# A hybrid mLSTM and delta-rule block: high and low part of the tokens in one moving operand of 512 columns

## The chip, the cores and the metric

The kernel runs on one core of a Trainium2 chip. The metric is the time of one execution on the device in microseconds (us); lower is better. "PE" is TensorE, "DVE" is VectorE, "ACT" is ScalarE, "POOL" is GpSimd and "SP" is SyncE, which issues most of the loads.

## What is computed

One layer of a bidirectional block on 256 tokens of width 2048, all in fp32:

```
h    = RMSNorm(x) * (1 + scale_m) + shift_m          # scale, shift, gates from silu(c) @ ada_w
proj = h @ w_in                                      # 2048 x 18512
y_a  = (sigmoid(a_o) * norm(biMLSTM(a_q, a_k, a_v, gates))) @ w_branch_a
qkv  = silu(conv5(b_qkv))                            # centred depthwise convolution, 5 taps
y_b  = (norm(biGatedDelta(qkv, gates)) * silu(b_z)) @ w_branch_b
x    = x + gate_m * ((g_a * y_a + g_b * y_b) @ w_out)
x    = x + gate_f * SwiGLU(RMSNorm(x) * (1 + scale_f) + shift_f)
out  = RMSNorm(x)
```

The delta rule (GDN) has 16 heads of width 128, the mLSTM 4 heads with keys of 256 and values of 512.

## The kernel before

A product of two fp32 matrices is made of three products in the faster type fp32r. Each operand is split into a high part (rounded to fp32r) and a low part (what is left): `hh` and `hl` for the tokens, `wh` and `wl` for the weights. The sum is hh·wh + hl·wh + hh·wl. For weights, ACT makes `wh` by a copy and DVE makes `wl` by a subtraction.

There are two kinds of job for a product with weights:

- `tjob`: the tokens are stationary (128 of them at a time), the weights move, 512 columns in one pass. It serves the projections that stay by token (z, v, o and the merge gates `ma`, `mb`), and later all products of the branches and the FFN.
- `fjob` (products by feature): the weights are stationary, 128 features at a time, and the 256 tokens move. The result is 128 features x 256 tokens in one half of a PSUM bank of 512 fp32. Its contraction over 2048 runs in 16 blocks, two halves of 8, and each half is one step of the job. Of these jobs there are 36 for q, k and v of the GDN heads 4 to 15 (`b_job`, tiles `acc_b`, `raw_b`, `wh_b`, `wl_b`) and 13 for q and k of the mLSTM heads (`a_qk`, tiles `acc_a` and so on). Heads 0 to 3 are made differently, in the first stage, by the product of L564 (`first`), which works on the unsplit fp32 `x`.

`woven` reorders the columns of the moving operand, so that the two halves of the tokens alternate. What is in the bank is therefore in alternating order, and the eviction reads it with a stride of two.

What follows an `fjob` is its `done`. For a GDN head that is `gdn_conv`: ACT copies the bank into `pad` (L336); ACT makes the middle tap of the convolution, `cv` (L339); DVE adds four more taps to it (L341); and later, as a function kept back in `behind` and called by `settle`, ACT makes the activation (L344) into `kq` or `vf`. `gdn_phase1` of the head takes these up: PE transposes `vf` (L612, tile `vps`), ACT squares `kq`. For the mLSTM, `keep_f` copies the bank into `ev` (L365, shown as `ev_a`), and ACT issues the store of it to DRAM.

The stages: first x is normalised and the first heads are made (to about 200 us). Then, to about 810 us, the GDN heads are worked through in groups of four. Their chain of small steps (phase 1, inversion, blocks, phase 2) would leave PE idle, so jobs are pulled in between: `stream` runs the b jobs of the next two heads and `fill` takes steps of the jobs in `rest`, in numbers written out by hand (`second`, `after`, `last`). Meanwhile `ada_parts` loads the rest of the modulation weights, 1 MB at a time, and DVE reduces each against the row of silu(c) (L114, 2.29 us each). From 965 us on follow the branches' products, the merge and the FFN, which have no `fjob`.

The order on PE is near that of the program. The order on DVE and ACT is fixed when the kernel is built, by a planner that goes by the order of the program, by when each instruction could start, and by its own costs; `order(...)` pins an instruction to its place in the program. Each engine then works its queue strictly in that order.

Of the kernel before, what the change touches and what calls it, by code (L numbers as in the profile page):

```python
# [10 lines left out]
F32R = mybir.dt.float32r  # L11
AF = mybir.ActivationFunctionType
ALU = mybir.AluOpType
PSUM = bass.MemoryType.PSUM

P = 128
T = 256
D = 2048
KB = D // P
# [6 lines left out]
GRP = 4  # L26
# [26 lines left out]
def hybrid_block(ctx: ExitStack, tc: tile.TileContext, xr, nfr, crow, pk_d, cst_d, ada2, ada4, win0, winb, wint, wba, wbb, wo, wgu, wd, out, dbg=None):  # L53
    nc = tc.nc
    V, S, G, PE = nc.vector, nc.scalar, nc.gpsimd, nc.tensor

    def pool(stack, name, bufs=1, **kw):
        return stack.enter_context(tc.tile_pool(name=name, bufs=bufs, **kw))
# [4 lines left out]
    g_ps = pool(ctx, "g_ps", 4, space=PSUM)  # L63
    sa, sx, sf = ExitStack(), ExitStack(), ExitStack()
    crp = pool(ctx, "crp")
    bigA = pool(sa, "bigA", 2, side="right")

    def big(p, dt, name):
        return p.tile([P, KB, T], dt, tag="b16", name=name)
# [106 lines left out]
    def fjob(name, src, done):  # L176

        ps = acc_ps.tile([P, 512], F32, tag="acc", name=f"acc_{name}")
        o = ps[:, :T]
        raw = raw_tile([P, KB, P], f"raw_{name}")  # L180
        nc.sync.dma_start(raw, src)
        for k0 in range(0, KB, 8):
            wh = st.tile([P, 8, P], F32R, tag="wh", bufs=3, name=f"wh_{name}_{k0}")
            wl = st.tile([P, 8, P], F32R, tag="wl", bufs=3, name=f"wl_{name}_{k0}")
            S.activation(wh, raw[:, k0 : k0 + 8], AF.Copy)  # L185
            settle()
            V.tensor_tensor(wl, raw[:, k0 : k0 + 8], wh.bitcast(F32), ALU.subtract)  # L187
            for k in range(8):
                kk = k0 + k
                PE.matmul(o, wh[:, k], woven(hh[:, kk]), start=kk == 0, stop=False)  # L190
                PE.matmul(o, wh[:, k], woven(hl[:, kk]), start=False, stop=False)  # L191
                PE.matmul(o, wl[:, k], woven(hh[:, kk]), start=False, stop=kk == KB - 1)  # L192
            if k0:
                pump()
                done(o.rearrange("p (c h) -> p h c", h=2))
            yield True

    def woven(a, n=2):

        return a.rearrange("p (h c) -> p c h", h=n)  # L200
# [95 lines left out]
    inst_d = [tc.dram_tile([64, 32, 32], F32, name=f"inst_d{g}") for g in range(NH_B // GRP)]  # L296
    inv_d = [tc.dram_tile([32, 4, 16, 32], F32, name=f"inv_d{g}") for g in range(NH_B // GRP)]

    hh = big(bigA, F32R, "hh")
    hl = big(bigA, F32R, "hl")  # L300

    evp = pool(sa, "evp", side="right")
    fr = pool(sf, "fr", side="right")
# [6 lines left out]
    for i in range(NP_):  # L310
        pd = fr.tile([P, T + 4], F32, name=f"pad{i}")
# [7 lines left out]
        order(G.memset(al[:, :, 0:8], 0.0))  # L319
        order(G.dma_start(al[:, :, 8:], alpha_d[:, h].partition_broadcast(P)))  # L320

    def gdn_conv(h, j, ps):

        if j == 0:
            kq = fr.tile([P, 2, T], F32, tag="kq", bufs=2, name=f"kq{h}")
            vf = fr.tile([P, T], F32, tag="vf", bufs=2, name=f"vf{h}")
            parts[h] = (kq, vf)
            if h == 1:
                decay_load(h)
        kq, vf = parts[h]  # L330
        cb = (16 + h, h, 32 + h)[j]
        w = [pk[:, PK_CONV + 5 * cb + i : PK_CONV + 5 * cb + i + 1] for i in range(5)]
        pd = pads[npad[0] % NP_]
        npad[0] += 1
        if ps is not None:
            S.activation(pd[:, 2 : T + 2].rearrange("p (h c) -> p h c", h=2), ps, AF.Copy)  # L336
        settle(1)
        cv = fr.tile([P, T], F32, tag="cv", bufs=2, name=f"cv{h}_{j}")
        S.activation(cv, pd[:, 2 : T + 2], AF.Copy, scale=w[2])  # L339
        for i in (0, 1, 3, 4):  # L340
            V.scalar_tensor_tensor(cv, pd[:, i : i + T], w[i], cv, ALU.mult, ALU.add)  # L341

        def end():
            order(S.activation(kq[:, j] if j < 2 else vf, cv, AF.Silu))  # L344
            if ps is None:
                evict(3 * h + j + 1 + NP_)

        behind.append(end)
# [11 lines left out]
        return done  # L360

    def keep_f(dst, name):
        def done(ps):
            ev = evp.tile([P, T], F32, tag="evf", bufs=2, name=f"ev_{name}")
            S.activation(ev.rearrange("p (h c) -> p h c", h=2), ps, AF.Copy)  # L365
            S.dma_start(dst, ev)
        return done

# [5 lines left out]
        return tjob(f"z{g}", [wint[g, u] for u in range(4)], hh, hl, done, early)  # L374

    def b_job(h, j):
        return fjob(f"b{h}_{j}", winb[3 * (h - GRP) + j], lambda ps: gdn_conv(h, j, ps))

    def a_qk(h, j):
        return fjob(f"a{h}_{j}", winb[36 + 4 * h + j], keep_f(kq_d[h][j], f"a{h}_{j}"))  # L380
# [115 lines left out]
    with ExitStack() as s0:  # L496
        w0 = pool(s0, "w0")

        x = w0.tile([P, KB, T], F32, name="x")
        ss = w0.tile([P, 2], F32, name="ssx")  # L500
        rows = w0.tile([P, T], F32, name="rows")
        xt = []
        for t in range(2):
            xt.append(w0.tile([P, D + 2], F32, tag="ra", bufs=5, name=f"xt{t}"))
            order(nc.sync.dma_start(xt[t][:, :D], xr[:, t]))

        junk = hl.rearrange("p b t -> p (b t)")
        c_row(0)
        order(S.activation(junk[:, :D], xt[0][:, :D], AF.Square, accum_out=ss[:, 0:1]))
        for g in (1, 2, 3):  # L510
            c_row(g)
        order(V.scalar_tensor_tensor(junk[:, D : 2 * D], xt[1][:, :D], 1.0, xt[1][:, :D], ALU.mult, ALU.mult, accum_out=ss[:, 1:2]))
        order(S.activation(ss, ss, AF.Sqrt, bias=epsc, scale=1.0 / D))

        def loads(b):
            ra = [w0.tile([P, D + 2], F32, tag="ra", bufs=5, name=f"ra{b}_{i}") for i in range(2)]
            raw = st.tile([P, N0, P], F32, tag="raw", bufs=3, name=f"raw0_{b}")
            for i in range(2):
                order(nc.sync.dma_start(ra[i], ada2[b, :, i]))
            order(nc.sync.dma_start(raw, win0[b]))  # L520
            return ra, raw

        def scale(b, ra):
            m2 = w0.tile([P, 2], F32, tag="m2", bufs=3, name=f"m2_{b}")
            f = pk[:, PK_NMIX + b : PK_NMIX + b + 1]
            order(V.scalar_tensor_tensor(ra[0], ra[0], f, row_c, ALU.mult, ALU.mult, accum_out=m2[:, 0:1]))
            return m2

        def shift(ra, m2):
            order(V.scalar_tensor_tensor(ra[1], ra[1], 1.0, row_c, ALU.mult, ALU.mult, accum_out=m2[:, 1:2]))  # L530

        ra, raw = loads(0)
        m2 = scale(0, ra)
        order(V.reciprocal(ss, ss))
        dg = w0.tile([P, T], F32, name="dgx")
        for t in range(2):
            order(V.tensor_scalar(dg[:, t * P : (t + 1) * P], ident, ss[:, t : t + 1], None, ALU.mult))
        shift(ra, m2)
        for b2 in range(KB // 2):
            px = gps(f"pxx{b2}")  # L540
            for e in range(2):
                for t in range(2):
                    order(PE.transpose(px[:, e * T + t * P : e * T + (t + 1) * P], xt[t][:, (2 * b2 + e) * P : (2 * b2 + e + 1) * P], ident))
            order(S.activation(x[:, 2 * b2 : 2 * b2 + 2], px.rearrange("p (e t) -> p e t", e=2), AF.Copy))
        prow = acc_ps.tile([P, 512], F32, tag="acc", name="prow")
        order(PE.matmul(prow[:, :T], ones, dg, start=True, stop=True))
        order(S.activation(rows, prow[:, :T], AF.Copy))
        banks = [acc_ps.tile([P, 512], F32, tag="acc", name=f"first{i}") for i in range(4)]
        banks += [gps(f"first{i}") for i in range(4, 8)]
        first = [banks[o // 2][:, (o % 2) * T : (o % 2 + 1) * T] for o in range(N0)]  # L550
        for b in range(KB):
            if b:
                ra, raw = loads(b)
                m2 = scale(b, ra)
            order(V.scalar_tensor_tensor(x[:, b], x[:, b], m2[:, 0:1], rows, ALU.mult, ALU.mult))
            if b:
                shift(ra, m2)
            order(S.activation(x[:, b], x[:, b], AF.Identity, bias=m2[:, 1:2]))  # L558
            order(S.activation(hh[:, b], x[:, b], AF.Copy))
            for bb in ((b - 1,) if b < KB - 1 else (b - 1, b)):  # L560
                if bb >= 0:
                    order(V.tensor_tensor(hl[:, bb], x[:, bb], hh[:, bb].bitcast(F32), ALU.subtract))
            for o in range(N0):
                PE.matmul(  # L564
                    first[o], raw[:, o], x[:, b], start=b == 0 and o % 2 == 0, stop=b == KB - 1 and o % 2 == 1
                )


        zj = z_job(0, 3)
        next(zj)  # L570
        fills[:] = [zj] + rest
        zz = w0.tile([P, T], F32, name="zz")
        for i, _ in enumerate(gates(w0, zz, first)):
            fill(2 if i in (2, 3, 4, 6, 8, 9, 10) else 1)
# [707 lines left out]
    left, right = slice(0, 256), slice(256, 512)  # L1282
# [120 lines left out]
    for j in range(FB // 4):  # L1403
# [4 lines left out]
        for e2 in range(2):  # L1408
            px = gps(f"pxf{j}_{e2}")
            for e in range(2):  # L1410
                f = 2 * e2 + e
                for t in range(2):
                    PE.transpose(px[:, e * T + t * P : e * T + (t + 1) * P], sg[:, t, f * P : (f + 1) * P], ident)
            b = 4 * j + 2 * e2
# [35 lines left out]
    for g in range(4):  # L1450
        c = slice(g * 512, (g + 1) * 512)
# [119 lines left out]
```

## Time and profile before

| what | before |
|---|---|
| time, median of 3 runs | 1991.46 us (1991.42 to 1999.04) |
| the profiled execution | 1994.34 us, span 1992.4 us |
| PE busy (matmuls) | 1937.3 us, 97% of the span |
| weight loads of PE (PEld) | 1708.8 us, 86% |
| DVE busy | 1407.0 us, 71% |
| ACT busy | 1032.8 us, 52% |
| POOL busy | 116.4 us, 6% |
| share of PE in the chain that ended last | 76% |
| granted clock of PE | 0.991 |

"Busy" counts the time in which at least one instruction of the engine is under way. Matmuls overlap one another, so the duration of one is longer than the interval at which they start; the interval is what a product costs when many follow each other. A line such as `L190 PE MATMUL acc_b<-hh,wh_b 128*128 128x256 f32 x576 | 163.4, 284 | 0.4 <-ACT wh_b L185 0.4` means: line 190, on PE, output `acc_b` from `hh` and `wh_b`, weights of 128x128, output 128x256, 576 times; 163.4 us busy, 284 ns on average; PE was idle for 0.4 us before them, waiting for ACT's `wh_b`. In a list of waits, "PEld vps L612 <- ACT vf L344: 11.5, 8, 4.8" means that the weight loads of L612 waited for ACT's `vf` for 11.5 us in all, 8 times, at most 4.8 us. In a timeline the first two numbers are the start and the duration in us.

### The profile page before, as it was taken

What the parts mean: (1) busy time and instruction counts of PE and PEld (TensorE: products, weight loads), DVE (VectorE), ACT (ScalarE), POOL (GpSimd) and SP (SyncE); (2) the same over time, 40 slices, a digit from 0 to 9 for tenths busy, and PEclk for the clock granted to TensorE, in tenths of its full rate; (3) what the DMA queues carried; (4) which work ended last, traced back from release to release, by engine and by line L of the source; (5) the groups of instructions that cost most, each with busy time, mean ns of one, the idle gap of its engine ahead of it and who ended that gap; (6) DMA issues with size and microseconds to landing.
All of it is one profiled execution on the core that took longest, in us unless ns stands there. A gap on an engine that the chain in (4) does not pass through costs nothing.

```text
span 1992.4 us, 27101 instructions
## 1 busy us (share of the span) xinstructions
PE 1937.3 (97%) x10418; PEld 1708.8 (86%) x10418; DVE 1407.0 (71%) x2067; ACT 1032.8 (52%) x1557; POOL 116.4 (6%) x211
## 2 busy tenths in 40 slices
PE   8999999999999999999999999999999999999998
PEld 6878889998898899889787888888888888888886
DVE  6778887887878798867476878765666665555554
ACT  3137647765666576555444544554444444444444
POOL 0001210111001101010100000200000000000000
PEclk9999999999999999999999999999999999999999
DMA  9987676655667666587786888566676675565653
GB/s 399 420 338 232 190 250 231 222 182 199 232 191 231 222 235 210 197 278 265 255 303 230 351 300 325 176 239 247 235 268 237 234 269 194 200 212 201 210 194 145
DMA packets 78962, 485.64 MB, mean 244 GB/s; under 512 B 10585, under 2 KB 15969, under 8 KB 24433
## 3 DMA queue, kind: packets, MB, share of 16 engines
q1 hardware_dynamic: 63216, 450.69, 62.6%
q0 software_dynamic: 8160, 17.88, 4.0%
q10 hardware_dynamic: 7458, 15.36, 2.0%
q8 instruction: 81, 1.33, 0.3%
q14 instruction: 47, 0.39, 0.1%
HBM read 467.07 MB, written 16.82 MB: 243 GB/s over the span
## 4 chain that ended last, share of the span: by engine, by line
PE 76%; DVE 10%; DMA 8%; ACT 2%; issue 2%; POOL 0%; ACTq 0%; SPq 0%; DVEq 0%; POOLq 0%
PE acc_gt L238 4%; PE acc_gt L237 4%; PE acc_gt L239 4%; PE acc_up L238 4%; PE acc_up L237 4%; PE acc_up L239 4%; PE acc_d L237 4%; PE acc_d L238 4%; PE acc_d L239 4%; DMA ra<-ada 3%; PE acc_o L239 2%; PE acc_o L237 2%; PE acc_o L238 2%; DMA ada<-ada 2%; PE acc_b L190 2%
## 5 line engine op out<-in xcount | busy, mean ns | idle before, releaser
L218 DVE TENSOR_TENSOR wl_d<-raw_d,wh_d 128x1024 fp32r<-128x1024 f32 x88 | 107.7, 1225 | 105.9 <-ACT wh_d L216 105.9
L218 DVE TENSOR_TENSOR wl_up<-raw_up,wh_up 128x1024 fp32r<-128x1024 f32 x88 | 107.7, 1225 | 100.3 <-ACT wh_up L216 100.3
L218 DVE TENSOR_TENSOR wl_gt<-raw_gt,wh_gt 128x1024 fp32r<-128x1024 f32 x88 | 108.2, 1229 | 79.6 <-ACT wh_gt L216 79.5
L190 PE MATMUL acc_b<-hh,wh_b 128*128 128x256 f32 x576 | 163.4, 284 | 0.4 <-ACT wh_b L185 0.4
L192 PE MATMUL acc_b<-hh,wl_b 128*128 128x256 f32 x576 | 160.2, 278 | 1.0 <-DVE wl_b L187 0.9
L191 PE MATMUL acc_b<-hl,wh_b 128*128 128x256 f32 x576 | 159.6, 277 | 0.0
L216 ACT ACTIVATE wh_d<-raw_d 128x1024 fp32r<-128x1024 f32 x88 | 93.0, 1057 | 126.3 <-PE acc_d L238 117.6
L114 DVE SCALAR_TENSOR_TENSOR ada<-ada,crow 128x2048 f32<-128x2048 f32 x64 | 146.4, 2288 | 14.8 <-DMA ada<-ada 14.7
L216 ACT ACTIVATE wh_gt<-raw_gt 128x1024 fp32r<-128x1024 f32 x88 | 92.9, 1056 | 118.6 <-PE acc_gt L238 71.0
L216 ACT ACTIVATE wh_up<-raw_up 128x1024 fp32r<-128x1024 f32 x88 | 92.8, 1055 | 108.1 <-PE acc_up L238 77.1
L237 PE MATMUL acc_gt<-wh_gt,hfh 128*128 128x512 f32 x352 | 135.5, 385 | 0.6 <-ACT hfh L1358 0.6
L238 PE MATMUL acc_gt<-wh_gt,hfl 128*128 128x512 f32 x352 | 135.2, 384 | 0.0
L239 PE MATMUL acc_gt<-wl_gt,hfh 128*128 128x512 f32 x352 | 134.0, 381 | 0.0
L237 PE MATMUL acc_up<-wh_up,hfh 128*128 128x512 f32 x352 | 133.4, 379 | 0.0
L238 PE MATMUL acc_up<-wh_up,hfl 128*128 128x512 f32 x352 | 133.4, 379 | 0.0
L239 PE MATMUL acc_up<-wl_up,hfh 128*128 128x512 f32 x352 | 133.4, 379 | 0.0
L237 PE MATMUL acc_d<-wh_d,ffh 128*128 128x512 f32 x344 | 130.5, 379 | 0.0
L238 PE MATMUL acc_d<-wh_d,ffl 128*128 128x512 f32 x344 | 130.5, 379 | 0.0
L239 PE MATMUL acc_d<-wl_d,ffh 128*128 128x512 f32 x344 | 130.4, 379 | 0.0
L564 PE MATMUL first<-x,raw 128*128 128x256 f32 x512 | 114.5, 382 | 7.6 <-ACT x L558 7.6
L564 PEld LDWEIGHTS first<-x,raw 128*128 128x128 f32 x512 | 96.0, 190 | 26.1 <-ACT x L558 13.6
L192 PEld LDWEIGHTS acc_b<-hh,wl_b 128*128 128x128 f32 x576 | 111.7, 194 | 1.7 <-DVE wl_b L187 1.7
(383 smaller groups left out, 5283.6 us busy)
## 6 DMA issues: line engine op xcount, KB each, us to landing
ada<-ada SPq DMA_DIRECT2D x64, 1024.0 KB, 5.0
raw_gt<-wgu SPq DMA_DIRECT2D x44, 1024.0 KB, 5.0
raw_up<-wgu SPq DMA_DIRECT2D x44, 1024.0 KB, 4.9
raw_d<-wd SPq DMA_DIRECT2D x44, 1024.0 KB, 4.9
raw_b<-winb SPq DMA_DIRECT2D x36, 1024.0 KB, 5.2
ra<-ada SPq DMA_DIRECT2D x32, 1025.0 KB, 15.7
raw<-win SPq DMA_DIRECT2D x16, 1024.0 KB, 14.5
raw_z<-wint SPq DMA_DIRECT2D x16, 1024.0 KB, 5.3
```

The source lines that it names most:

```text
L114: order(V.scalar_tensor_tensor(raw, raw, 1.0, row_c[:, :D], ALU.mult, ALU.mult, accum_out=mod[:, c : c + 1]), room[0][3] > 1)
L190: PE.matmul(o, wh[:, k], woven(hh[:, kk]), start=kk == 0, stop=False)
L191: PE.matmul(o, wh[:, k], woven(hl[:, kk]), start=False, stop=False)
L192: PE.matmul(o, wl[:, k], woven(hh[:, kk]), start=False, stop=kk == KB - 1)
L216: order(S.activation(wh, raws[u][:, k0 : k0 + 2], AF.Copy), early)
L218: order(V.tensor_tensor(wl, raws[u][:, k0 : k0 + 2], wh.bitcast(F32), ALU.subtract), early)
L237: order(PE.matmul(ps[t], xh[:, kk, c], woven(wh[:, k]), start=kk == 0, stop=False), early and steps > 1)
L238: PE.matmul(ps[t], xl[:, kk, c], woven(wh[:, k]), start=False, stop=False)
L239: PE.matmul(ps[t], xh[:, kk, c], woven(wl[:, k]), start=False, stop=kk == last)
L564: PE.matmul(first[o], raw[:, o], x[:, b], start=b == 0 and o % 2 == 0, stop=b == KB - 1 and o % 2 == 1)
```

## The change

`hh` and `hl` become the two halves of one tile `h2` of 16 blocks x 2 parts x 256 tokens. In `fjob`, the two products of each block that have `wh` as weights are replaced by one, whose moving operand is the block's 2 x 256 columns and whose output is the whole bank: hh·wh goes to the first half and hl·wh to the second. The product with `wl` still moves 256 columns of `hh` and adds to the first half. When the job is done, ACT copies the first half as before, and DVE then adds the second half to the copy. For that, `done` gets two arguments, `gdn_conv` and `keep_f` each get an addition, and in `keep_f` the store follows it. The scratch `junk` of the first stage lies in `h2` instead of `hl`. `tjob` works on `hh` and `hl` as before.

```diff
-    bigA = pool(sa, "bigA", 2, side="right")
+    bigA = pool(sa, "bigA", side="right")
...
         ps = acc_ps.tile([P, 512], F32, tag="acc", name=f"acc_{name}")
-        o = ps[:, :T]
...
-                PE.matmul(o, wh[:, k], woven(hh[:, kk]), start=kk == 0, stop=False)
-                PE.matmul(o, wh[:, k], woven(hl[:, kk]), start=False, stop=False)
-                PE.matmul(o, wl[:, k], woven(hh[:, kk]), start=False, stop=kk == KB - 1)
+                PE.matmul(
+                    ps.rearrange("p (x c h) -> p x c h", x=2, h=2), wh[:, k],
+                    h2[:, kk].rearrange("p x (h c) -> p x c h", h=2), start=kk == 0, stop=False,
+                )
+                PE.matmul(ps[:, :T].rearrange("p (c h) -> p c h", h=2), wl[:, k], woven(hh[:, kk]), start=False, stop=kk == KB - 1)
             if k0:
                 pump()
-                done(o.rearrange("p (c h) -> p h c", h=2))
+                done(*(ps[:, i * T : (i + 1) * T].rearrange("p (c h) -> p h c", h=2) for i in range(2)))
...
-    hh = big(bigA, F32R, "hh")
-    hl = big(bigA, F32R, "hl")
+    h2 = bigA.tile([P, KB, 2, T], F32R, name="h2")
+    hh, hl = h2[:, :, 0], h2[:, :, 1]
...
-    def gdn_conv(h, j, ps):
+    def gdn_conv(h, j, ps, low=None):
...
         if ps is not None:
-            S.activation(pd[:, 2 : T + 2].rearrange("p (h c) -> p h c", h=2), ps, AF.Copy)
+            inner = pd[:, 2 : T + 2].rearrange("p (h c) -> p h c", h=2)
+            S.activation(inner, ps, AF.Copy)
+            V.tensor_tensor(inner, inner, low, ALU.add)
...
-        def done(ps):
+        def done(ps, low):
             ev = evp.tile([P, T], F32, tag="evf", bufs=2, name=f"ev_{name}")
-            S.activation(ev.rearrange("p (h c) -> p h c", h=2), ps, AF.Copy)
+            evh = ev.rearrange("p (h c) -> p h c", h=2)
+            S.activation(evh, ps, AF.Copy)
+            V.tensor_tensor(evh, evh, low, ALU.add)
             S.dma_start(dst, ev)
...
-        return fjob(f"b{h}_{j}", winb[3 * (h - GRP) + j], lambda ps: gdn_conv(h, j, ps))
+        return fjob(f"b{h}_{j}", winb[3 * (h - GRP) + j], lambda *ps: gdn_conv(h, j, *ps))
...
-        junk = hl.rearrange("p b t -> p (b t)")
+        junk = h2.rearrange("p b x t -> p (b x t)")
```

## The prediction

> **What bounds the kernel now.** I read the page first, then the groups of instructions with their shapes, the stretch in which the changed jobs run, the matmuls one by one, and the waits of that stretch.
>
> ```profile
> span 1992.4 us, 27101 instructions
> PE 1937.3 (97%) x10418; PEld 1708.8 (86%) x10418; DVE 1407.0 (71%) x2067; ACT 1032.8 (52%) x1557; POOL 116.4 (6%) x211
> PE 76%; DVE 10%; DMA 8%; ACT 2%; issue 2%; POOL 0%; ACTq 0%; SPq 0%; DVEq 0%; POOLq 0%
> L190 PE MATMUL acc_b<-hh,wh_b 128*128 128x256 f32 x576 | 163.4, 284 | 0.4 <-ACT wh_b L185 0.4
> L190 PE MATMUL acc_a<-hh,wh_a 128*128 128x256 f32 x208 | 59.9, 288 | 0.0
> L564 PE MATMUL first<-x,raw 128*128 128x256 f32 x512 | 114.5, 382 | 7.6 <-ACT x L558 7.6
> L643 PE MATMUL ks<-kqh 128*128 128x512 f32 x24 | 9.2, 384 | 0.0
> ```
>
> PE is the bound: 97% of the span, 76% of the chain. The change touches 576 + 208 = 784 steps of the inner loop (36 jobs `acc_b`, 13 jobs `acc_a`, 16 blocks each). The 284 ns of a 256-column product say little, since products overlap; what counts is the interval from start to start:
>
> ```profile
> 314.63 0.28 PE L191 MATMUL acc_b<-hl,wh_b 128*128 128x256 f32 x1
> ...
> 317.08 0.28 PE L192 MATMUL acc_b<-hh,wl_b 128*128 128x256 f32 x1
> ...
> 1499.74 0.38 PE L237 MATMUL acc_gt<-wh_gt,hfh 128*128 128x512 f32 x1
> ...
> 1503.85 0.38 PE L238 MATMUL acc_gt<-wh_gt,hfl 128*128 128x512 f32 x1
> ```
>
> From 314.63 to 317.08 lie 22 intervals: 2.45 / 22 = 111.4 ns for 256 columns. From 1499.74 to 1503.85 lie 19: 4.11 / 19 = 216.3 ns for 512. So 512 columns cost almost as much in one pass as in two, and the change can win only the small difference. The stretch it wins it in:
>
> ```profile
> 300.00:810.00 510.00, 487.08 (x3463) 456.93 (x3461) 413.47 (x812) 338.94 (x639) 52.05 (x103) 0.99 0.65 216
> 810.00:965.00 155.00, 149.80 (x913) 136.68 (x914) 109.18 (x174) 82.83 (x141) 13.87 (x25) 0.98 0.72 251
> PEld vps L612 <- ACT vf L344: 11.5, 8, 4.8
> PEld acc_mb L239 <- DVE wl_mb L218: 3.3, 3, 1.2
> PEld acc_ma L239 <- DVE wl_ma L218: 2.5, 2, 1.5
> PEld acc_z L239 <- DVE wl_z L218: 1.8, 4, 1.0
> PEld acc_b L192 <- DVE wl_b L187: 1.7, 4, 1.0
> ACT wh_ma L216 <- PE acc_a L191: 13.2, 7, 3.1
> ACT wh_a L185 <- PE acc_a L191: 7.0, 5, 1.8
> ```
>
> The columns of the first two lines are PE, PEld, DVE, ACT and POOL busy, then clock and DMA. PE is idle for 28 of 665 us here; DVE is busy for 413.5 + 109.2 = 522.7 us (79%). The longest wait of PE's weight loads is for `vf`, the convolved and activated v part of a GDN head: 11.5 us at 8 places. The low weight parts from DVE cost it 3.3 + 2.5 + 1.8 + 1.7 = 9.3 us more. ACT, on the other hand, waits for PE to free its weight buffers: it runs ahead.
>
> **The change part by part.** *Fewer, wider products.* Per block two products of 256 columns become one of 512: 2 x 111.4 - 216.3 = 6.5 ns less. Over 784 blocks that is 5.1 us of PE work, in a stretch where PE is the bound. As many weight loads go too, but those lie beside the products and are in the interval already. I take the 5.1 us whole; the least good end, a wide pass that runs slower, is a rival below. The Trainium skill ("TensorE: Matmul & The Clock Gate", section "Back-to-back issue gap") gives the interval as N / 2.4 + 2.5 ns, so that two products merged into one would save only the fixed 2.5 ns, in all an estimate of 2.0 us; this trace has 111.4 where that rule has 109.2, and 216.3 where it has 215.8. By the rule the sum below would come out at +8.6 instead of +5.5 us.
>
> *One addition more per job on DVE.* The two halves of the bank are added after ACT has copied the first. The same shape from a bank read at the same stride of two is in the trace:
>
> ```profile
> L654 DVE TENSOR_TENSOR at<-ks,dec 128x256 f32<-128x256 f32 x16 | 6.7, 416 | 0.0
> ```
>
> 36 + 13 = 49 additions at 0.416 us are 20.4 us of DVE work. DVE does not bound the stretch (79% becomes about 82%), so the work as such costs nothing, but its idle time falls from 142 to 122 us. If PE's waits for low weight parts grow as that idle time shrinks, 9.3 us x 142 / 122 is 1.6 us more. From below this is bounded by 0 (other work fills the gaps), from above by a quarter of the 20.4 us, about 5, if one addition in four delays a weight part that PE is waiting for. I take 1.6, since those waits are so few (13 in all above).
>
> *The v chain gets one engine change longer.* Before, ACT copies the bank into `pad` and goes straight on to the first tap `cv` (L339); then come four taps on DVE (L341) and the activation to `vf` on ACT, on which PE's transposes wait. Now ACT copies, DVE adds, ACT makes the first tap, DVE the other four: the chain enters DVE's queue twice. One head of before:
>
> ```profile
> 513.24 0.36 ACT L336 ACTIVATE pad<-acc_b 128x256 f32<-128x256 f32 x1
> ...
> 514.02 0.49 ACT L339 ACTIVATE cv<-pad,pk 128x256 f32<-128x256 f32 x1
> ...
> 512.42 2.36 DVE L187 TENSOR_TENSOR wl_b<-raw_b,wh_b 128x1024 fp32r<-128x1024 f32 x2 [0.34 <-ACT wh_b L185]
> 514.69 0.48 DVE L341 SCALAR_TENSOR_TENSOR cv<-pad,pk,cv 128x256 f32<-128x256 f32 x1
> 515.09 2.29 DVE L114 SCALAR_TENSOR_TENSOR ada<-ada,crow 128x2048 f32<-128x2048 f32 x1
> ...
> 517.30 0.48 DVE L341 SCALAR_TENSOR_TENSOR cv<-pad,pk,cv 128x256 f32<-128x256 f32 x1
> 517.70 0.69 DVE L609 TENSOR_TENSOR kql<-kq,kqh 128x512 fp32r<-128x512 f32 x1
> 518.30 1.00 DVE L341 SCALAR_TENSOR_TENSOR cv<-pad,pk,cv 128x256 f32<-128x256 f32 x2
> 519.33 0.42 ACT L344 ACTIVATE vf<-cv 128x256 f32<-128x256 f32 x1 [3.26 <-DVE cv L341]
> ```
>
> Here DVE is busy until 514.7 with weight parts, and ACT's first tap lies wholly beside that. With the change the addition takes the place at 514.7, and the first tap (0.49) begins only after it: 0.42 + 0.49 = 0.9 us later, where PE is already waiting. It could cost nothing, if DVE does the 2.29 us for `ada` (which it has to do anyway) during the first tap; it could cost 0.42 + 2.29 = 2.7 us, if a piece for `ada` that was not in the chain before gets in between. I take 0.9, which is what the chain's own rows give. At the 8 places where PE waits already, this is 8 x 0.9 = 7.2 us. The k and q chains (24 of the 36) gain the same 0.9 us, but none of them is in PE's waits above: their results are used a job or more later, so I cost them at nothing. Behind ACT's wait for the addition are queued the casts of the weights (`wh`), which run ahead of PE.
>
> *The a jobs.* There ACT issues the store of `ev_a` itself. Before, that followed ACT's own copy; now it waits for DVE's addition, and the casts of the weights wait behind it. 13 times an addition, with one weight part ahead of it, are 13 x (0.42 + 1.2) = 21 us of ACT's time at most; ACT's own waits for PE in these jobs, 13.2 + 7.0 us, cover it. If they do so entirely it is 0; I take 1.8 us for places where they don't.
>
> *One tile for both parts of the tokens* moves nothing: the same bytes, and both parts are complete before the first of these jobs starts.
>
> Sum: -5.1 + 1.6 + 7.2 + 1.8 = **+5.5 us**. The profiled execution took 1994.34 us (its span 1992.4); it would become 1999.8. The median of the runs shown is 1991.46, 0.14% under the profiled one, so I forecast 1991.46 + 5.5 = **1997.0 us**, +0.3%. With 4 to 11 us for the chain's places it lies at 1994 to 2001.
>
> **The rivals.** *A: the chain hides it.* The planner puts DVE's other work into the gap that the first tap leaves, and the chain costs nothing: -5.1 + 1.6 = -3.5, or 1988 us. For it: every one of the chains shows other DVE work between its taps. Against: those pieces stand there already, and PE waits all the same. In a twentieth of the cases a new order also takes away over 6 us of the 20.8 us of waits above, and it is faster than 1981.5.
>
> *B: the second entry into DVE's queue takes a whole piece each time.* The addition, and then the taps again, find a weight part (1.2 us) or an `ada` piece (2.29) ahead of them. At 2.7 us a place: 8 x 2.7 = 21.6, and the sum is -5.1 + 1.6 + 21.6 + 1.8 = +19.9, or 2011 us. It decides from about 1.5 us a place: then 8 x 1.5 - 1.7 is +10. For it speaks that DVE is 81% busy in the first of the two windows (413 of 510); and a long wait costs twice, because PE's clock falls behind it:
>
> ```profile
> 549.32 0.44 PE L612 MATMUL vps<-cst,vf 128*128 128x128 f32 x2 [4.62 <-ACT vf L344]
> 400.00:500.00 100.00, 96.32 (x574) 86.99 (x574) 76.59 (x162) 59.33 (x102) 13.38 (x26) 1.00 0.58 191
> 500.00:600.00 100.00, 93.13 (x777) 91.19 (x776) 82.02 (x159) 67.22 (x138) 6.95 (x14) 0.97 0.64 212
> ```
>
> After the wait of 4.62 us the granted clock of those 100 us is 0.97 instead of 1.00, that is 3 us lost. Two more of these would make 2017. Against it: in the head above the queue was empty of other work at the right moment.
>
> *C: the wide pass doesn't run at full speed*, so that the change does not do what it says. Its moving operand has one level more than that of L643, which takes two strided rows in 512 columns at 384 ns, no longer than the others (0.38). The nearest bad row is L564: 256 columns in 382 ns, as long as 512 elsewhere. If the new pass took twice its time, that is 784 x 216 ns = 169 us, or 2166 us. The order in which the bank is written stays contiguous, and L643 shows strides in the moving operand to be free, so this has little chance. The Trainium skill ("PSUM — Partial Sum Buffer", section "Specifications (TRN2)") says that any non-contiguous access pattern slows matmuls significantly; it gives no size, and no run here shows it for a pattern such as this.
>
> **How the numbers follow.** A difference of under 0.5% (10 us) is about what a measurement of this kernel cannot tell from no change: the three runs of before reach from 1991.42 to 1999.04. Chances: the forecast 0.46, A 0.18, B 0.33, C 0.03. Slower by over 0.5% (above 2001.4) is B and C, 0.36; faster by as much is the twentieth out of A, 0.05; the rest, 0.59, is within. The range from 1986 to 2014 leaves out C, a quarter of B (0.09) and 0.07 of A.
>
> **What would show it.** In the profile after, L190 should have groups of 128x512 x576 and x208 with starts 216 ns apart, L191's are gone, and the remaining product keeps 111 ns; DVE gains 36 and 13 additions of 0.42 us and about 20 us in all; PE's wait for `vf` grows from 11.5 to about 19 us. If that wait stays at 11 us, A was right; if it passes 25 us or the clock of another stretch falls below 1.00, B was. Starts 400 ns apart would mean C. I would be wrong altogether if PE's idle time grew at waits other than `vf` and the weight parts, or if the order on DVE changed so much that single groups can't be compared.

## The result, and the profile after

| | before | after |
|---|---|---|
| median | 1991.44 us (22 runs, 1980.52 to 2005.74) | 1997.3 us (22 runs, 1992.12 to 2003.65) |
| ratio to before, 95% interval | | 1.0028 [1.0015, 1.0042] |
| profiled execution, span | 1994.34 us, 1992.4 us | 2003.65 us, 2001.6 us |

The change makes the kernel slower by 0.28%, or 5.6 us. The forecast was 1997.0. The total came out; most of its terms did not, as the profile shows. The profiled execution of after was the slowest of its 22, so that the two profiled executions lie 9.2 us of span apart and not 5.6. First the page of after, with the groups of the new inner loop, each a row of output and input, busy time, mean of one, and idle time ahead of it:

```profile
span 2001.6 us, 25570 instructions
PE 1936.6 (97%) x9634; PEld 1683.2 (84%) x9634; DVE 1421.6 (71%) x2116; ACT 1030.2 (51%) x1555; POOL 116.4 (6%) x211
L189 PE MATMUL acc_b<-h,wh_b 128*128 128x512 f32 x576 | 199.6, 394 | 0.2 <-ACT wh_b L184 0.2
L193 PE MATMUL acc_b<-h,wl_b 128*128 128x256 f32 x576 | 161.1, 280 | 5.0 <-DVE wl_b L186 5.0
```

784 products and as many weight loads are gone, and DVE has 49 instructions more. The same stretch as in the prediction, in windows (PE, PEld, DVE, ACT, POOL busy, then clock, DMA share and GB/s):

```profile
300.00:810.00 510.00, 484.82 (x2799) 434.56 (x2798) 424.25 (x844) 335.68 (x636) 52.35 (x103) 0.98 0.64 215
810.00:965.00 155.00, 144.48 (x772) 128.30 (x771) 112.33 (x186) 80.31 (x132) 13.84 (x25) 0.96 0.68 242
```

PE lost 2.3 us of busy time in the first window (487.08 before) and 5.3 in the second (149.80 before), and the clock fell from 0.99 and 0.98 to 0.98 and 0.96. A loss of more than twice the size in the shorter window points to a place, not to a load that is spread out. The timeline of PE shows that the wide pass itself is what was hoped for:

```profile
315.58 0.38 PE L189 MATMUL acc_b<-h,wh_b 128*128 128x512 f32 x1
315.80 0.27 PE L193 MATMUL acc_b<-h,wl_b 128*128 128x256 f32 x1
...
317.55 0.38 PE L189 MATMUL acc_b<-h,wh_b 128*128 128x512 f32 x1
```

From 315.58 to 317.55 lie 6 blocks: 328 ns each, where three products of 111.4 made 334. That is 6 ns, and 4.6 us over 784 blocks. (The median over all blocks that follow one another directly is 335 ns in before and 328 ns in after.) The waits of 300 to 975 us in after (us in all, times, longest):

```profile
PEld vps L617 <- ACT vf L347: 10.9, 8, 2.3
PEld acc_b L193 <- DVE wl_b L186: 6.7, 6, 2.6
PEld p L791 <- ACT X L785: 6.6, 1, 6.6
ACT cv L342 <- DVE pad L339: 8.6, 11, 1.3
```

PE's wait for `vf`, which was to grow from 11.5 to 19 us, stayed at 10.9. The wait of the b jobs for their low weight parts grew from 1.7 to 6.7. And there is a wait that before does not have: 6.6 us once, at `p` (L791), in the second window, next to one of 6.1 us of DVE for an `ada` load.

The place, in the timeline of before and then of after. L704 and L731 (`inv_d`, `cg`) take the finished inversion through DRAM, issued by POOL; L114 is DVE's piece for `ada`, which waits for its load (L132), and `Et` (L776, L781) is the small transpose on which ACT's `X`, and then PE's `p`, wait:

```profile
859.61 2.00 POOL L726 DMA_DIRECT2D cg<-inv_d  x4 [5.56 <-DMA inv_d<-uu]
...
865.41 0.54 POOL L945 DMA_DIRECT2D vt<-v_d  x1
871.91 0.33 SPq L132 DMA_DIRECT2D ada<-ada  x1
879.02 2.29 DVE L114 SCALAR_TENSOR_TENSOR ada<-ada,crow 128x2048 f32<-128x2048 f32 x1 [1.48 <-DMA ada<-ada]
```

```profile
865.38 2.00 POOL L731 DMA_DIRECT2D cg<-inv_d  x4 [3.22 <-DMA inv_d<-uu]
...
871.02 0.53 POOL L950 DMA_DIRECT2D vt<-v_d  x1
873.46 0.33 SPq L132 DMA_DIRECT2D ada<-ada  x1
884.13 2.29 DVE L114 SCALAR_TENSOR_TENSOR ada<-ada,crow 128x2048 f32<-128x2048 f32 x1 [6.11 <-DMA ada<-ada]
886.34 0.31 DVE L781 STREAM_TRANSPOSE Et<-p 128x128 f32<-128x128 f32 x1
```

In before POOL's loads are issued from 859.6, the last of them at 865.4, 6.5 us ahead of the `ada` load, which is reduced 7.1 us after its issue. In after they come 5.8 us later, up to 871.6, and the `ada` load close behind them takes 10.7 us. DVE stands for 6.11 us at its piece, and `Et`, queued behind it, is late. What that costs, in the window from 868 to 900 of before and then of after:

```profile
868.00:900.00 32.00, 31.51 (x166) 27.84 (x165) 22.20 (x26) 21.09 (x39) 0.00 (x0) 1.00 0.83 302
```

```profile
868.00:900.00 32.00, 25.79 (x123) 22.40 (x122) 17.65 (x24) 18.07 (x32) 3.56 (x6) 0.84 0.72 250
```

PE loses 5.7 us of busy time. Its clock is at half for 10.2 us, and PE is busy for 5.37 of them (windows in the last section), which loses 2.7 us more: 8.4 us. PE's steps say the same: from the start of `p<-R,cc` to that of `p<-X,pt` before takes 13.80 us (874.66, L764, to 888.46, L798) and after 22.15 (876.31, L769, to 898.46, L803). That is most of the 9.2 us between the two profiled executions. Why POOL's loads are later is seen in the last inversion, which DVE works through almost without a pause (first and last of its `uu` steps and what stands between them, before and then after):

```profile
819.10 0.21 DVE L713 TENSOR_TENSOR uu<-uu,utmp 64x30 f32<-64x30 f32 x1
...
851.34 0.18 DVE L713 TENSOR_TENSOR uu<-uu,utmp 64x30 f32<-64x30 f32 x1
```

```profile
821.60 0.20 DVE L718 TENSOR_TENSOR uu<-uu,utmp 64x30 f32<-64x30 f32 x1
...
844.85 0.41 DVE L370 TENSOR_TENSOR ev_a<-ev_a,acc_a 128x256 f32<-128x256 f32 x1
850.83 0.41 DVE L370 TENSOR_TENSOR ev_a<-ev_a,acc_a 128x256 f32<-128x256 f32 x1
856.27 0.41 DVE L370 TENSOR_TENSOR ev_a<-ev_a,acc_a 128x256 f32<-128x256 f32 x1
...
859.46 0.18 DVE L718 TENSOR_TENSOR uu<-uu,utmp 64x30 f32<-64x30 f32 x1
```

From the first start to the last, 32.2 us became 37.9. The order on DVE now has 14 low weight parts in this stretch instead of 11, and three additions of a jobs: 3 x 1.2 + 3 x 0.41 = 4.8 us of the 5.6; once, at 843.70, DVE also stands for 1.38 us until ACT has made a `wh_a`. DVE is 71% busy over the kernel, but an inversion is bound by it. Windows over two inversions of before, and over the last one of after, have it busy for 95%, 95% and 92%:

```profile
439.10:472.70 33.60, 32.04 (x148) 27.42 (x147) 31.96 (x73) 17.32 (x19) 2.25 (x4) 1.00 0.60 204
818.90:851.50 32.60, 32.37 (x220) 30.20 (x219) 30.94 (x74) 15.57 (x18) 2.23 (x4) 1.00 0.65 215
```

```profile
821.40:859.60 38.20, 38.20 (x202) 34.15 (x201) 35.28 (x80) 18.96 (x21) 2.23 (x4) 1.00 0.63 217
```

### The profile page after: what moved, and what is told of

Its sections match the earlier page's. It is cut to its first block, busy times and chain, and to the rows that moved or that the text cites. A ratio compares the mean times of both kernels' runs of the same rounds, so it can differ in the third digit from the quotient of the medians.

```text
span 2001.6 us, 25570 instructions
## 1 busy us (share of the span) xinstructions
PE 1936.6 (97%) x9634; PEld 1683.2 (84%) x9634; DVE 1421.6 (71%) x2116; ACT 1030.2 (51%) x1555; POOL 116.4 (6%) x211
## 4 chain that ended last, share of the span: by engine, by line
PE 76%; DVE 10%; DMA 7%; ACT 4%; issue 2%; POOL 0%; ACTq 0%; SPq 0%; DVEq 0%; POOLq 0%
PE acc_gt L239 4%; PE acc_gt L238 4%; PE acc_gt L240 4%; PE acc_up L238 4%; PE acc_up L240 4%; PE acc_up L239 4%; PE acc_d L240 4%; PE acc_d L238 4%; PE acc_d L239 4%; PE acc_b L189 3%; DMA ra<-ada 2%; PE acc_o L240 2%; PE acc_o L238 2%; PE acc_o L239 2%; PE first L569 2%; PE acc_a L189 2%
## 5 line engine op out<-in xcount | busy, mean ns | idle before, releaser
L189 PE MATMUL acc_b<-h,wh_b 128*128 128x512 f32 x576 | 199.6, 394 | 0.2 <-ACT wh_b L184 0.2
L193 PE MATMUL acc_b<-h,wl_b 128*128 128x256 f32 x576 | 161.1, 280 | 5.0 <-DVE wl_b L186 5.0
L114 DVE SCALAR_TENSOR_TENSOR ada<-ada,crow 128x2048 f32<-128x2048 f32 x64 | 146.2, 2285 | 11.2 <-DMA ada<-ada 10.8
L189 PEld LDWEIGHTS acc_b<-h,wh_b 128*128 128x128 f32 x576 | 111.3, 193 | 14.7 <-ACT wh_b L184 0.3
L193 PEld LDWEIGHTS acc_b<-h,wl_b 128*128 128x128 f32 x576 | 112.8, 196 | 6.8 <-DVE wl_b L186 6.7
```

The costliest lines, as they stand in the source:

```text
L114: order(V.scalar_tensor_tensor(raw, raw, 1.0, row_c[:, :D], ALU.mult, ALU.mult, accum_out=mod[:, c : c + 1]), room[0][3] > 1)
L189: PE.matmul(ps.rearrange("p (x c h) -> p x c h", x=2, h=2), wh[:, k], h2[:, kk].rearrange("p x (h c) -> p x c h", h=2), start=kk == 0, sto ...
L193: PE.matmul(ps[:, :T].rearrange("p (c h) -> p c h", h=2), wl[:, k], woven(hh[:, kk]), start=False, stop=kk == KB - 1)
```

## The experiments

All ratios are to the kernel before on the same chip, with a 95% interval.

**1. No additions.** Both `V.tensor_tensor(..., low, ALU.add)` are taken out of after; the result then lacks hl·wh of these jobs.

```
-            V.tensor_tensor(inner, inner, low, ALU.add)
-            V.tensor_tensor(evh, evh, low, ALU.add)
```

> The changed kernel without the 49 additions: the wide pass is there, the second half of the bank is never added (hl x wh of these jobs is left out of the result). Theory of the prediction (the wide pass gains 5.1 us, the additions and what waits for them cost the rest): 5 us under before, about 1986. Rival 1 (the order that the planner makes anew is what costs, not the additions): as slow as the changed kernel, 1997. Rival 2 (the wide pass gains nothing, the kernel is bound by chains here): 1991.

1978.41 us, 0.9921 [0.9898, 0.9944]. The additions, with what hangs on them and the new order, are what costs; but the kernel without them is 15.7 us faster than before, and not 5. That is a miss of size, taken up in 9 to 12.

**2. Two narrow passes, additions kept.**

```
-                PE.matmul(ps.rearrange(...x=2, h=2), wh[:, k], h2[:, kk].rearrange(...), start=kk == 0, stop=False)
+                PE.matmul(ps[:, :T], wh[:, k], woven(hh[:, kk]), start=kk == 0, stop=False)
+                PE.matmul(ps[:, T:], wh[:, k], woven(hl[:, kk]), start=False, stop=False)
```

> The changed kernel with two passes of 256 columns into the two halves of the bank instead of one of 512; the additions stay. Theory of the prediction: the wide pass is worth 5.1 us, so this loses it: 1997 + 5 = 2002, 10.6 us over before. Rival 2 (the wide pass gains nothing): 1997, as the changed kernel.

2003.24 us, 1.0045 [1.0028, 1.0061]. Beside the additions the wide pass is worth 0.17%, 3.4 us, by the point estimates. The interval overlaps with that of after, so this run alone can't tell the 5 us of the theory from nothing.

**3. The same addition in before, with no reader.** DVE adds `pad` (or `ev`) and the bank into the unused half of the bank; nothing reads the sum, and only the next use of the bank has to wait for it.

```
             S.activation(inner, ps, AF.Copy)
+            V.tensor_tensor(spare, inner, ps, ALU.add)
```

> The kernel before, with an addition of the same shape on DVE after each of the 49 jobs, whose result goes into the unused half of the bank and is read by nobody: the load on DVE without a longer chain. Theory of the prediction: the load alone costs 1.6 us of the 10.6, so about 1993. Rival 3 (the additions cost by their place in DVE's queue: DVE stands still until ACT has copied, and weight parts wait behind; the chain behind the addition is not what costs): as much as with the chain, 2000 to 2002.

2002.12 us, 1.0043 [1.0028, 1.0057]: as much as in run 2 (1.0045), which has the same narrow passes and the addition in the chain. The difference is 0.4 us, with an uncertainty of some 4; the 7.2 us of the prediction's main cost, the longer v chain, lie outside. The waits of this kernel from 300 to 975 us say the same, and those from 868 to 900 show the place again:

```profile
PEld vps L616 <- ACT vf L346: 4.8, 7, 1.2
```

```profile
PEld p L790 <- ACT X L784: 6.0, 1, 6.0
DVE ada L114 <- DMA ada<-ada: 5.5, 1, 5.5
```

The wait for `vf` is less than half that of before, and the kernel is slower all the same.

**4. The change in the 36 GDN jobs alone.** For names with "a" the two narrow passes of before, and no addition.

```
+                if name[0] == "a":
+                    PE.matmul(ps[:, :T], wh[:, k], woven(hh[:, kk]), start=kk == 0, stop=False)
+                    PE.matmul(ps[:, :T], wh[:, k], woven(hl[:, kk]), start=False, stop=False)
+                else:
...
-            V.tensor_tensor(evh, evh, low, ALU.add)
```

> The change in the 36 jobs of the GDN heads alone; the 13 jobs of the mLSTM heads take three passes of 256 columns and no addition, as before. Theory of the prediction: it loses 1.35 us of the gain (208 of 784 blocks) and is spared 1.8 us of ACT's wait and 0.4 of DVE's load: about 1996, as the changed kernel within 1 us. Rival 4 (ACT's wait for DVE ahead of the store in the 13 jobs is the main cost): 1990 or less.

1992.02 us, 0.9999 [0.9981, 1.0016]. With the 13 a jobs as before, for which the prediction had 1.8 us, nothing is left of the loss.

**5. Only the four a2 jobs as before.** As in 4, with `name[:2] == "a2"`; the three additions that after has in its last inversion are of these jobs.

> The changed kernel with 4 of its 49 jobs, a2_0 to a2_3, as before (three passes, no addition): three of these additions stand inside the last inversion on DVE, which took 32.6 us in the kernel before, without them, and 38.2 in the changed one. Theory S (one site: DVE is the bound inside the inversion, so the additions there make it longer; the loads behind it then meet a load for ada, and PE waits 6.2 us): 6 to 10 us under the changed kernel, 1988 to 1991. Rival L (the load of the additions costs everywhere alike): 4/49 of it, 1 us, so about 1997.

1991.87 us, 0.9998 [0.9978, 1.0019]. Four of 49 jobs take the whole loss away, where rival L had 1 us for them. An addition's price is not the same for every job.

**6. After, with the `ada` load held back at the place**, and **7. the same in before**, as a control.

```
-                held[0] = n < 4
+                held[0] = n < (7 if g == 3 and p == 0 else 4)
```

> The changed kernel, in which no new piece of ada is begun in the first six steps after the last inversion (before: three), so that DVE does not stand before the transposition Et waiting for that piece's load. Theory S: the inversion stays long, but PE's wait of 6.2 us and the half clock behind it go: 5 to 9 us less, 1988 to 1992. Rival L: 1997.

> The control for the one with ada held back: the kernel before with the same hold. Theory S: in the kernel before DVE waited 1.5 us there and PE not at all, so nothing changes: 1991 within 2 us. If it gains as much as the changed kernel does, the hold is a gain by itself and says nothing on the change.

After with the hold: 1989.14 us, 0.9979 [0.9959, 0.9999]. Before with it: 1991.71, 0.9995 [0.9976, 1.0013]. The edit does nothing by itself that could be measured, and takes 0.5%, 9.8 us, from after. The windows of after with the hold, of the last inversion and of the place:

```profile
818.00:856.30 38.30, 38.30 (x202) 34.25 (x201) 35.37 (x80) 18.95 (x21) 2.23 (x4) 1.00 0.62 217
868.00:900.00 32.00, 32.00 (x172) 28.46 (x171) 20.06 (x27) 22.92 (x41) 0.24 (x1) 1.00 0.77 282
```

The inversion is as long as in after, with PE busy through all of it; at the place PE is busy for 32.00 of 32 us at full clock. From `p<-R,cc` to `p<-X,pt` it now takes 13.04 us (872.94 to 885.98) instead of 22.15. So the longer inversion costs nothing by itself that shows here; it costs by bringing two loads together. The same window in the kernels of 2, 3, 4 and 5:

```profile
868.00:900.00 32.00, 26.67 (x132) 23.30 (x131) 18.84 (x25) 18.69 (x33) 5.83 (x11) 0.89 0.75 267
```

```profile
868.00:900.00 32.00, 26.38 (x122) 22.71 (x121) 16.76 (x24) 17.68 (x31) 6.06 (x11) 0.89 0.77 274
```

```profile
868.00:900.00 32.00, 31.63 (x167) 27.93 (x166) 23.13 (x28) 22.41 (x40) 0.00 (x0) 1.00 0.81 304
```

```profile
868.00:900.00 32.00, 30.94 (x163) 27.35 (x162) 22.06 (x29) 21.21 (x39) 0.00 (x0) 1.00 0.79 292
```

Of these and the kernels above, the three with the stall (after, 2, 3) stand at 1.0028 to 1.0045; those without it at or under 1.000. Two that follow, 8 and 11, are above 1.000 by their point estimates without this stall, so it is not the only way to lose.

**8. The addition on POOL.** ACT copies both halves, POOL adds.

```
+            S.activation(lwh, low, AF.Copy)
+            G.tensor_tensor(inner, inner, lwh, ALU.add)
```

> The changed kernel with the addition on POOL: ACT copies both halves of the bank to SBUF (49 copies of 0.37 us more) and POOL adds them. Theory (the additions cost by their place in DVE's queue, as the run with the unread addition showed; a longer chain does not): it keeps most of what the run without additions gained, 1980 to 1988. Rival (the chain's length does cost, or POOL's queue, which stands waiting for long loads and stores, holds the chain up): 1997 or more.

2002.38 us, 1.0043 [1.0022, 1.0063], a miss. The place is nearly clean (PE busy 29.36 of 32 us at clock 1.00), but here the chain did become longer. The waits of 300 to 975 us:

```profile
ACT cv L345 <- POOL pad L342: 20.1, 18, 3.0
PEld vps L623 <- ACT vf L350: 13.5, 9, 3.0
```

ACT waits 20.1 us for POOL's additions at the first tap, where it waited 8.6 us for DVE's in after. That this chain is all of the cost is not shown: ACT also makes 49 copies more.

**9 to 12. Is the surplus of run 1 made of such places?** In before, PE waits 4.8 us at 544 us for a `vf` whose activation stands on ACT behind a late weight load, which was issued after an `ada` load (534.64 and 539.88) into the same ring of buffers; the kernel of run 1 does not. Run 9 is before with the pieces of that time held back, run 10 is after with that and the hold of 6, run 11 is after with a short hold in every group, run 12 joins the cures of 5 and 6.

```
+                held[0] = n < (10 if g == 1 and p == 0 else 4)                # 9, from before
+                held[0] = n < ((4, 10, 4, 7)[g] if p == 0 else 4)             # 10, from after
+                held[0] = n < (7 if p == 0 else 4)                            # 11, from after
+                held[0] = n < (7 if g == 3 and p == 0 else 4)                 # 12, from run 5
```

> The kernel before with one line changed: in group 1 no piece of the ada load is issued during the first pair of heads. In the trace of before, at 544 us, PE waits 4.9 us (a weight load for an a job was issued late, behind an ada piece in the same buffers), and then runs 6.8 us at half clock; the kernel without additions has neither. Theory T (the 15.7 us that the kernel without additions gains hold such places beside the 5 us of the wide pass): without the piece this kernel gains 4.9 + 3.4 = 8.3 us, ratio 0.996. Rival D (the additions' load on DVE is what was saved, all along the stretch, and the place is an accident that costs nothing elsewhere): ratio 1.000.

> The kernel after with the ada load held back longer in group 3 (as in the run at 0.998) and in group 1 too. Theory T: its trace has no long wait at 544 us, but 2.8 us at 515 (a low weight part late, beside an ada piece) with half clock behind it; without those pieces 3 to 5 us less than with the hold in group 3 alone, ratio 0.996. Rival D: 0.998, as with the hold in group 3 alone.

> The kernel after with the ada load held back a little longer (n below 7 rather than 4) in the first pair of every group. Theory T: what counts is whether a piece meets a load that somebody waits for, so this does at the late place what the hold in group 3 did and changes little else: 0.998. Rival D: the same. A ratio under 0.995 or over 1.001 would say that a small move of the pieces anywhere shifts the time by as much as the change does.

> The kernel after with the hold in group 3, and the four a2 jobs made as before (two passes of 256, no addition). Theory T: the last inversion is back at 32.6 us instead of 38.2, and the ada piece meets nothing; the second cure adds only what PE still waits behind the inversion, 2 to 4 us: ratio 0.9965. If the inversion's length were the cost by itself, 5.6 us less than the hold alone: 0.995. If the meeting with the ada piece was all of it, nothing more: 0.998.

| run | us | ratio |
|---|---|---|
| 9 | 1992.01 | 0.9987 [0.9964, 1.0011] |
| 10 | 1993.08 | 0.9996 [0.9972, 1.0020] |
| 11 | 1997.31 | 1.0017 [0.9996, 1.0039] |
| 12 | 1992.77 | 0.9995 [0.9973, 1.0017] |

Theory T asked for 0.996 in 9 and 10, and neither interval reaches it; rival D's 1.000 for 9 and 0.998 for 10 lie inside. The windows from 530 to 560 and from 560 to 700 us say where the gain of 9 went, before first and run 9 below it:

```profile
530.00:560.00 30.00, 25.38 (x194) 24.98 (x192) 22.53 (x52) 16.26 (x40) 3.49 (x7) 0.89 0.62 199
560.00:700.00 140.00, 131.75 (x856) 119.60 (x856) 112.01 (x213) 85.45 (x150) 16.88 (x33) 1.00 0.68 221
```

```profile
530.00:560.00 30.00, 30.00 (x265) 29.79 (x264) 24.94 (x60) 20.64 (x50) 6.96 (x14) 1.00 0.58 166
560.00:700.00 140.00, 127.90 (x735) 115.14 (x734) 106.33 (x198) 76.48 (x134) 13.44 (x26) 0.93 0.64 217
```

The place was cured: PE busy 30.00 instead of 25.38 us, clock 1.00 instead of 0.89. In the next 140 us it was given back, with 3.9 us less busy time and the clock at 0.93. New waits stand there, in run 9 from 560 to 700 us:

```profile
PEld acc_ma L237 <- ACT wh_ma L216: 3.6, 1, 3.6
PEld p L764 <- DVE R L733: 3.4, 1, 3.4
```

The first is again a weight copy of ACT, the second a step of the delta rule on DVE; what made each of them late was not followed further. Run 12 gained nothing over run 6, which fits its third case (the meeting of the two loads was all of it) and not the other two. Run 11 was to be 0.998 and is 1.0017, above its own bound of 1.001 by the point estimate, although it has no stall at the late place either (13.04 us between the two `p` steps): against run 6, moving the pieces in groups 0 to 2 cost it 0.38%, more than the 0.28% of the change itself. Run 6, which beats both kernels by its point estimate, is therefore to be read with that in mind: its interval ends at 0.9999, and runs 10 and 12, close to it, are at 0.9996 and 0.9995.

## Why the prediction was right, and where it was not

*The gain (-5.1 us)* was right where it can be read directly: 6 ns a block in the timeline, 7 by the medians, which is 4.6 to 5.5 us. The runs agree loosely: 3.4 us between after and run 2, and -4.2 us (0.9979) in run 6, where the stall is gone but the additions are still paid. The Trainium skill ("TensorE: Matmul & The Clock Gate", section "Back-to-back issue gap") would have 2.0 us by its rule; the intervals of the runs, several us wide, can't tell 2 from 5, but the spacing of the products, 328 ns for a block instead of 334, agrees with the trace of before and not with a saving of 2.5 ns.

*Rival C (a slow wide pass)* fell: 0.22 us from the wide pass to the next product, 0.11 from that to the next wide one. The Trainium skill's sentence on non-contiguous patterns ("PSUM — Partial Sum Buffer", section "Specifications (TRN2)") does not show here in the moving operand: that of this pass has several levels with a stride, and it takes no more than the 216 ns of a plain one, within the rounding of the timeline. The sentence stands in a table on PSUM, and PSUM is written in contiguous order here; no run tests it for that side.

*The v chain (+7.2)*, the largest term, failed. PE's wait for `vf` went from 11.5 to 10.9, and an addition without readers (run 3) cost as much as one in the chain (run 2). The step took one head in which DVE was free at the right moment and priced all 8 places by it; the planner makes a new order, and the waits there are set by that order. (By the prediction's own test, a wait that stays at 11 us means rival A; A's 1988 is close to run 6, after without the stall, at 1989.14. Its sign for B, the clock of another stretch below 1.00, is there too, 0.84 from 868 to 900: a small step did stand behind a whole `ada` piece, but it was `Et`, once, and not the v chain at 8 places.)

*DVE's load (+1.6) and the a jobs (+1.8).* These two were mis-sized, and for one reason: the load was averaged over 665 us. The four waits for low weight parts that the prediction lists rose by 3.6 us (9.3 to 12.9) and not by 1.6, and the larger cost was at none of them. DVE's 79% is made of inversions that fill it to 95% and of slack between them. Three additions and three weight parts inside the last inversion pushed its end by 5.6 us against its start, POOL's loads with it, into an `ada` load. Runs 5 and 6 price this meeting at 0.30% and 0.49%, 6 to 10 us; runs 10 and 12, which do not have it either, at 0.32% and 0.33%. For the a jobs the prediction looked at ACT's store and its cover, and not at where on DVE the addition falls.

*The sum (+5.5)* came out at +5.6, and that is luck: 10.6 us of costs, most of them in the wrong places, stand against 8.4 at one place that it did not name, and against gains and losses elsewhere that it did not name either. The wait of before at 544 us is one of these: after has PE busy for 29.00 of the 30 us from 530 to 560, at clock 1.00, where before has 25.38 at 0.89. What it won there it lost in part nearby, at a low weight part 2.6 us late at 518 us. The prediction named what would make it wrong, a growth of PE's idle time at waits other than `vf` and the weight parts: that is what the profile shows.

*What stays open* is the surplus of run 1: 15.7 us without additions, where run 6, with additions and without the stall, gains 4.2. So the additions take some 11 us beside the stall, or run 1's order happens to be a good one. Run 9 shows that one place cured is not enough; whether it is DVE's load all along (rival D, which runs 9 and 10 allow) or the order was not separated. A part can be placed: between two steps `p<-X,pt`, at 505.99 and 576.86 us in before, lie 70.9 us, in run 1 63.7 (502.71 to 566.39), in run 9 61.7 (507.27 to 569.00). So 7.2 of the 17.8 us between the profiled executions of before and run 1 lie at the place that Theory T named; run 9 won more there and lost it later, and run 1 did not lose it. No run held the order fixed while the additions were taken out.

## What to carry to other kernels

Price added work on a half-idle engine by where it lands: look for the stretches where that engine runs without a pause, list what is issued when they end, and ask what that will meet when it comes later by the sum of the additions. A stall found in a trace is worth its length only if the work behind it is not waiting for something else; test it by moving one transfer, with the same move in the old kernel as a control. When a planner makes a new order for every variant, differences of some 0.3% between variants belong to the order as much as to the edit.

## What the runs showed of the hardware

A wait is paid again in PE's clock, and only for the time in which PE is busy. After the stall of after, the windows from 873.5 us on show 10.2 us at half clock, with PE busy for only 5.37 us of them, so that the clock falls while PE still waits, and 2.7 us are lost. Products of 512 columns start 0.43 us apart there (890.23, 890.65) and 0.22 behind it (893.70, 893.92):

```profile
873.50:883.10 9.60, 8.22 (x46) 7.08 (x44) 1.77 (x4) 7.00 (x12) 0.00 (x0) 1.00 0.97 367
883.10:893.30 10.20, 5.37 (x15) 4.46 (x16) 7.05 (x10) 5.16 (x12) 0.00 (x0) 0.50 0.60 227
```

Behind the wait of before at 544 us it was 6.8 us, with PE busy throughout, which loses 3.4:

```profile
549.80:556.60 6.80, 6.80 (x33) 6.80 (x33) 3.33 (x15) 4.23 (x8) 0.00 (x0) 0.50 0.19 75
```

An `ada` load of 1 MB was reduced 7.1 us after its issue when the last of POOL's loads had been issued 6.5 us before it, and 10.7 us after it when that was 2.4 us; the DMA engines were busy for 97% of the 9.6 us from 873.5 in which it waited.
